# Padding each high weight tile by 96 bytes, so that its five places start at five positions within 512 bytes of SBUF

## The chip, the cores and the metric

The kernel runs on one core of a Trainium2 chip. The metric is the device time of one execution in microseconds (us), lower is better. Three runs of the kernel before gave 1294.0, 1297.97 and 1297.98 us; their median, 1297.97 us, is the time before.

## The reference

A decoder trunk of two layers over 512 tokens of width 1024, all in float32. Layer 0 mixes tokens with stick-breaking attention (16 heads of 64), layer 1 with dilated sliding-window attention (three groups of 8 heads). Behind each mixer stands a gated feed-forward block with a causal convolution of width 3 over 2816 channels. Cut to what matters here, which is that nearly all work is products of activations with weights that are read once:

```python
def reference(x, ...):
    for i in range(DEPTH):                       # 2 layers
        hn = rms_norm(x, norm_gains[i, 0])
        if kind == 0:
            m = stick_breaking_attention(hn, sb_w_qkv[j], sb_w_o[j])     # hn @ w_qkv, ..., o @ w_o
        elif kind == 1:
            m = dilated_attention(hn, dil_w_qkv[j], dil_w_o[j], rel_bias)
        x = x + rms_norm(m, norm_gains[i, 1])
        f = conv_ffn(rms_norm(x, norm_gains[i, 2]), ffn_w_up[i], ffn_conv_w[i],
                     ffn_conv_b[i], ffn_w_down[i])                       # (silu(g) * u) @ w_down
        x = x + rms_norm(f, norm_gains[i, 3])
    return x
```

## The kernel before

Every weight matrix is cut on the host into 204 pieces of 128x1024 float32 (512 KB). A piece goes through class Weights in three steps. `load` fetches it by a DMA of the SP queue into one of three places `wraw`. `split` makes two parts of it: `wh`, the value rounded to the matrix engine's float32r format, by a copy on ACT (L77), and `wl`, the remainder raw minus `wh`, by a subtraction on DVE (L78). Each part has five places in SBUF (`n_high` is 5), which are used in turn. `next` hands a piece to the matmuls, cut along its row into 8 blocks of 128 or 2 blocks of 512 columns, and `done` splits the next piece and starts the load behind it.

A product is made of three matmuls that add into the same PSUM bank, high by high, high by low and low by high:

```python
def mm3(o, sH, sL, mH, mL, first, last):
    nc.tensor.matmul(o, sH, mH, start=first, stop=False)   # L202
    nc.tensor.matmul(o, sH, mL, start=False, stop=False)   # L203
    nc.tensor.matmul(o, sL, mH, start=False, stop=last)    # L204
```

The first operand of a matmul is held in the array: it is loaded ahead of each matmul by a weight load (PEld in the profile, 128x128). The second is streamed through it (512 columns, in one place 256). Two families follow from which side the weights stand on:

- Weights held, activations `hH`, `hL` streamed: `proj_f`, used for the projections to queries and keys (tiles `qk` in layer 0, `dqk` in layer 1) and for the wide half of the feed-forward block (`up`).
- Activations held, weights streamed: the values (`v`, with `hH`, `hL` held; `dv`, with `hH`, `hL` or their regrouped copies `hc` held), the output projections (`o`, `do`, with `oH`, `oL` or `doH`, `doL` held) and the narrow half of the feed-forward block (`dn`, with `gH`, `gL` held).

The program's order is that of the code: the attention of one pair of heads is slipped between the projections of the next, so that the matrix engine always has a projection at hand. The pieces are split several ahead of their use, as far as the five places go.

Tiles of one pool lie behind each other in SBUF. All the large ones have a length of a multiple of 512 bytes per partition, so that tiles of a pool start at the same position within 512 bytes. A row of a 128-column block is 512 bytes, one of 512 columns 2048 bytes, so every block of a tile also starts at that position. In the kernel before, `x`, `hH`, `hL`, `wraw`, `wh`, `wl` and `hc` all start at 352 within 512, and `oH`, `oL`, `doH`, `doL`, `gH`, `gL` at 288.

Of the kernel before, what the change touches and what calls it, by code (L numbers as in the profile page):

```python
# [10 lines left out]
F32 = mybir.dt.float32  # L11
F32R = mybir.dt.float32r
I32 = mybir.dt.int32
AF = mybir.ActivationFunctionType
ALU = mybir.AluOpType
# [3 lines left out]
P = 128  # L19
# [26 lines left out]
class Weights:  # L46
# [22 lines left out]
    def split(self):  # L69
        n = self.splitted  # L70
        if n >= len(self.srcs):
            return
        nc = self.nc
        raw = self.raw.pop(n)
        h = self.pool.tile([P, 1024], F32R, name=f"wh{n}", tag="wh", bufs=self.n_high)
        low = self.pool.tile([P, 1024], F32R, name=f"wl{n}", tag="wl", bufs=self.n_high)
        nc.scalar.copy(h, raw)  # L77
        nc.vector.tensor_tensor(low, raw, h[:].bitcast(F32), op=ALU.subtract)  # L78
        self.parts[n] = (h, low)
        self.splitted += 1  # L80

    def next(self, m):

        n = self.used
        self.used += 1
        h, low = self.parts[n]
        return (
            h[:].rearrange("p (k m) -> p k m", m=m),
            low[:].rearrange("p (k m) -> p k m", m=m),
        )  # L90

    def done(self, later=False):
# [14 lines left out]
def hybrid_trunk_kernel(  # L107
# [275 lines left out]
    with ExitStack() as c2:  # L383
# [7 lines left out]
        r_in = []  # L391
        bias = bias_vectors(ap.tile([P, 2 * 10 * P], F32, name="room", tag="at"))
        next(bias)
        keep_busy(6)
        turned(0, 0, ident, "in0")
# [36 lines left out]

        v_half(0)
        next(bias)
        v_half(1)
        nc.vector.tensor_copy(
# [588 lines left out]
```

## Time and profile before

| what | value |
|---|---|
| median of three runs | 1297.97 us (1294.0 to 1297.98) |
| the profiled execution's own time | 1296.61 us |
| its span, first to last instruction | 1294.8 us |
| TensorE matmul (PE) busy | 1268.5 us, 98% |
| TensorE weight load (PEld) busy | 1024.9 us, 79% |
| VectorE (DVE) busy | 767.8 us, 59% |
| ScalarE (ACT) busy | 554.5 us, 43% |
| mean granted TensorE clock | 0.989 of full speed |

The profiled execution took 1.81 us more than its span, and it lies 1.36 us under the median. A matmul's busy time is longer than its share of the engine, because matmuls overlap in the pipeline and their ends are modelled: the pace of the engine is read from the distance between the starts of two matmuls, in the view of instructions in order of time. That view gives starts in steps of 0.01 us, so a pace is read from two starts that lie far apart and the number of matmuls between them.

### The profile page before, as it was taken

The page shows a single profiled execution, that of the slowest core. Times are in us where ns is not written, and L with a number is a line of the kernel's source. Part 1 is how long each engine was busy: PE and PEld are TensorE (multiplying, and loading weights), DVE is VectorE, ACT ScalarE, POOL GpSimd, SP SyncE. Part 2 cuts the span into 40 slices and gives each one's busy share as a digit, 9 for nine tenths or more (in the row PEclk, how much of TensorE's full clock was granted, in tenths as well). Part 3 has the DMA queues.
Part 4 walks back from the last instruction along what each step waited for, and adds up shares of the span by engine and source line. Part 5 has one row for each costly group of instructions (what it writes and reads, how often), then busy time and mean ns, then how long its engine had stood idle before and what let it go on. Part 6 is the DMA issues. An engine that isn't in the chain of part 4 may idle for free.

```text
span 1294.8 us, 16912 instructions
## 1 busy us (share of the span) xinstructions
PE 1268.5 (98%) x6556; PEld 1024.9 (79%) x6556; DVE 767.8 (59%) x1425; ACT 554.5 (43%) x941; POOL 74.5 (6%) x169
## 2 busy tenths in 40 slices
PE   8998999999999999999999999999999999999997
PEld 6775776788888888888878877777888888888886
DVE  5266788378777777332663354455887777773324
ACT  6445556356444444221455243334654444442210
POOL 1000000000000000000260012300100000000000
PEclk8998999999999999999999999999999999999999
DMA  6541212243323324322463323330433322343311
GB/s 217 105 129 33 66 65 95 75 144 114 98 98 98 98 98 145 116 91 93 131 187 98 98 75 95 88 121 27 150 114 98 98 98 98 96 138 112 95 64 65
DMA packets 39760, 133.48 MB, mean 103 GB/s; under 512 B 6047, under 2 KB 7103, under 8 KB 39680
## 3 DMA queue, kind: packets, MB, share of 16 engines
q1 hardware_dynamic: 32400, 115.37, 27.6%
q0 software_dynamic: 7280, 17.03, 4.8%
q8 instruction: 51, 0.84, 0.3%
q14 instruction: 29, 0.24, 0.1%
HBM read 122.78 MB, written 9.60 MB: 102 GB/s over the span
## 4 chain that ended last, share of the span: by engine, by line
PE 94%; DVE 2%; ACT 2%; issue 1%; DMA 1%; SPq 0%; DVEq 0%; ACTq 0%
PE up L203 12%; PE up L202 12%; PE up L204 12%; PE dn L203 6%; PE dn L202 6%; PE dn L204 6%; PE dqk L202 4%; PE dqk L204 3%; PE dqk L203 3%; PE qk L202 2%; PE qk L204 2%; PE qk L203 2%; PE dv L202 2%; PE dv L204 2%; PE dv L203 2%; PE z L359 2%
## 5 line engine op out<-in xcount | busy, mean ns | idle before, releaser
L78 DVE TENSOR_TENSOR wl<-wraw,wh 128x1024 fp32r<-128x1024 f32 x204 | 249.5, 1224 | 218.5 <-ACT wh L77 215.9
L77 ACT CAST wh<-wraw 128x1024 fp32r<-128x1024 f32 x204 | 214.5, 1051 | 267.0 <-PE dn L204 137.8
L203 PE MATMUL up<-hL,wh 128*128 128x512 f32 (+1 forms) x768 | 285.4, 373 | 2.1 <-DVE hL L269 2.1
L202 PE MATMUL up<-hH,wh 128*128 128x512 f32 (+1 forms) x768 | 284.5, 374 | 1.1 <-ACT hH L268 1.1
L204 PE MATMUL up<-hH,wl 128*128 128x512 f32 (+1 forms) x768 | 284.8, 372 | 0.0
L203 PEld LDWEIGHTS up<-hL,wh 128*128 128x128 f32 x768 | 145.1, 189 | 27.6 <-DVE hL L269 2.8
L202 PEld LDWEIGHTS up<-hH,wh 128*128 128x128 f32 x768 | 143.9, 189 | 27.2 <-ACT hH L268 2.0
L204 PEld LDWEIGHTS up<-hH,wl 128*128 128x128 f32 x768 | 145.1, 189 | 25.2
L203 PE MATMUL dn<-wl,gH 128*128 128x512 f32 x352 | 138.7, 394 | 0.0
L202 PE MATMUL dn<-wh,gH 128*128 128x512 f32 x352 | 138.0, 392 | 0.0
L204 PE MATMUL dn<-wh,gL 128*128 128x512 f32 x352 | 136.6, 388 | 0.0
L607 DVE SCALAR_TENSOR_TENSOR up<-work,cw,up 128x510 f32<-128x510 f32 (+1 forms) x176 | 131.5, 751 | 5.0 <-ACT up L605 2.2
L604 DVE TENSOR_TENSOR work<-up,rows 128x512 f32<-128x512 f32 x88 | 60.1, 687 | 70.6 <-PE up L204 70.6
L202 PEld LDWEIGHTS dn<-wh,gH 128*128 128x128 f32 x352 | 66.1, 188 | 15.4
L202 PE MATMUL dqk<-hH,wh 128*128 128x512 f32 x192 | 77.8, 405 | 0.0
L204 PEld LDWEIGHTS dn<-wh,gL 128*128 128x128 f32 x352 | 66.1, 188 | 14.8
L203 PEld LDWEIGHTS dn<-wl,gH 128*128 128x128 f32 x352 | 66.2, 188 | 13.1
L204 PE MATMUL dqk<-hH,wl 128*128 128x512 f32 x192 | 75.1, 391 | 0.0
L203 PE MATMUL dqk<-hL,wh 128*128 128x512 f32 x192 | 75.0, 391 | 0.0
L605 ACT ACTIVATE up<-work,cb,cw 128x512 f32<-128x512 f32 x88 | 68.6, 781 | 11.6 <-DVE work L604 9.3
L618 ACT CAST gH<-work 128x512 fp32r<-128x512 f32 x44 | 27.2, 618 | 106.7 <-DVE work L617 106.7
L616 ACT ACTIVATE work<-up 128x512 f32<-128x512 f32 x44 | 26.3, 597 | 73.4 <-DVE up L607 73.3
(236 smaller groups left out, 1751.2 us busy)
## 6 DMA issues: line engine op xcount, KB each, us to landing
wraw<-in_up_dram SPq DMA_DIRECT2D x88, 512.0 KB, 3.5
wraw<-in_down_dram SPq DMA_DIRECT2D x44, 512.0 KB, 3.5
wraw<-in_dl_qk_dram SPq DMA_DIRECT2D x24, 512.0 KB, 3.5
wraw<-in_sb_qk_dram SPq DMA_DIRECT2D x16, 512.0 KB, 4.1
wraw<-in_dl_v_dram SPq DMA_DIRECT2D x12, 512.0 KB, 4.1
wraw<-in_sb_v_dram SPq DMA_DIRECT2D x8, 512.0 KB, 5.3
wraw<-in_sb_o_dram SPq DMA_DIRECT2D x8, 512.0 KB, 3.5
x<-x_away POOLq DMA_DIRECT2D x8, 512.0 KB, 3.8
```

What stands on the lines that cost most here:

```text
L77: nc.scalar.copy(h, raw)
L78: nc.vector.tensor_tensor(low, raw, h[:].bitcast(F32), op=ALU.subtract)
L202: nc.tensor.matmul(o, sH, mH, start=first, stop=False)
L203: nc.tensor.matmul(o, sH, mL, start=False, stop=False)
L204: nc.tensor.matmul(o, sL, mH, start=False, stop=last)
L359: nc.tensor.matmul(outs[h], lhs[r, :], rhs[r, :], start=True, stop=True, tile_position=(h * HD, 0))
L604: nc.vector.tensor_tensor(h, o, rows, op=ALU.mult)
L605: nc.scalar.activation(o, h, AF.Identity, bias=cb[:, f : f + 1], scale=cw[:, f, 2:3])
L607: nc.vector.scalar_tensor_tensor(o[:, : S - s], h[:, s:], cw[:, f, 2 - s : 3 - s], o[:, : S - s], op0=ALU.mult, op1=ALU.add,)
L616: nc.scalar.activation(g, og, AF.Silu)
L618: nc.scalar.copy(gH[:, f, :], u)
```

## The change

Each tile `wh` is allocated with 24 more columns (96 bytes) than it holds, and the code uses its first 1024. The rest of the diff moves the slicing `[:]` from the uses to the allocation.

```diff
-        h = self.pool.tile([P, 1024], F32R, name=f"wh{n}", tag="wh", bufs=self.n_high)
-        low = self.pool.tile([P, 1024], F32R, name=f"wl{n}", tag="wl", bufs=self.n_high)
+
+        h = self.pool.tile([P, 1024 + 24], F32R, name=f"wh{n}", tag="wh", bufs=self.n_high)[:, :1024]
+        low = self.pool.tile([P, 1024], F32R, name=f"wl{n}", tag="wl", bufs=self.n_high)[:]
         nc.scalar.copy(h, raw)
-        nc.vector.tensor_tensor(low, raw, h[:].bitcast(F32), op=ALU.subtract)
+        nc.vector.tensor_tensor(low, raw, h.bitcast(F32), op=ALU.subtract)
```

No instruction is added, taken away or moved: on every engine and queue the two programs have the same instructions with the same shapes in the same order, and the same waits. What differs is where tiles start. Positions within 512 bytes of a partition, as the two built programs have them:

| tiles | before | after |
|---|---|---|
| `x`, `qk`, `work`, `hH`, `hL`, `wraw` | 352 | 352 |
| `wh`, five places | 352 each | 352, 448, 32, 128, 224 |
| `wl`, five places | 352 each | 320 each |
| `hc` and the other temporaries, `dqk` of odd pairs | 352 | 320 |
| `oH`, `oL`, `doH`, `doL`, `gH`, `gL`, `v_sb` | 288 | 256 |

All that lies behind the five places of `wh` is 480 bytes further on, which is 32 bytes less within 512.

## Rows read from the trace of the kernel before

**Rows 1.** The page: busy time, share and instructions of each engine; then the chain's engines.
```profile
PE 1268.5 (98%) x6556; PEld 1024.9 (79%) x6556; DVE 767.8 (59%) x1425; ACT 554.5 (43%) x941; POOL 74.5 (6%) x169
...
PE 94%; DVE 2%; ACT 2%; issue 1%; DMA 1%; SPq 0%; DVEq 0%; ACTq 0%
```

**Rows 2.** Who waited for whom, PE alone: us in total, times, longest; the longest row.
```profile
PE o L517 <- ACT at L508: 4.3, 1, 4.3
```

**Rows 3.** Groups by shape: line, engine, tiles, shapes, count | busy us, mean ns | idle before.
```profile
L202 PE MATMUL up<-hH,wh 128*128 128x512 f32 x640 | 249.0, 389 | 0.0
...
L202 PE MATMUL dn<-wh,gH 128*128 128x512 f32 x352 | 138.0, 392 | 0.0
...
L202 PE MATMUL dqk<-hH,wh 128*128 128x512 f32 x192 | 77.8, 405 | 0.0
...
L202 PE MATMUL qk<-hH,wh 128*128 128x512 f32 x128 | 52.6, 411 | 0.0
...
L204 PE MATMUL up<-hH,wl 128*128 128x256 f32 x128 | 35.9, 287 | 0.0
...
L202 PE MATMUL v<-wh,hH 128*128 128x512 f32 x64 | 27.2, 425 | 0.8 <-ACT hH L268 0.8
L202 PE MATMUL o<-wh,oH 128*128 128x512 f32 x64 | 26.3, 411 | 0.0
...
L202 PE MATMUL dv<-wh,hc 128*128 128x512 f32 x64 | 25.2, 394 | 1.6 <-ACT hc L725 1.6
...
L202 PE MATMUL do<-wh,doH 128*128 128x512 f32 x32 | 13.3, 414 | 0.0
L202 PE MATMUL dv<-wh,hH 128*128 128x512 f32 x32 | 12.9, 404 | 0.0
```

**Rows 4.** The same view: the group that makes the low part of the weights.
```profile
L78 DVE TENSOR_TENSOR wl<-wraw,wh 128x1024 fp32r<-128x1024 f32 x204 | 249.5, 1224 | 218.5 <-ACT wh L77 215.9
```

**Rows 5.** Busy time by stretch: stretch, us, PE, PEld, DVE, ACT, POOL, clock, DMA share, GB/s.
```profile
292.00:519.00 227.00, 227.00 (x1033) 189.26 (x1032) 170.37 (x216) 105.67 (x133) 1.63 (x3) 1.00 0.33 107
```

**Rows 6.** Instructions in order of time (start, us each): PE in `up`, first and last of 181.
```profile
330.01 0.39 PE L203 MATMUL up<-hL,wh 128*128 128x512 f32 x1
...
370.81 0.39 PE L203 MATMUL up<-hL,wh 128*128 128x512 f32 x1
```

**Rows 7.** The same view: PE in `dv`, activations `hc` held, first and last of 175.
```profile
669.92 0.39 PE L202 MATMUL dv<-wh,hc 128*128 128x512 f32 x1
...
709.37 0.39 PE L202 MATMUL dv<-wh,hc 128*128 128x512 f32 x1
```

**Rows 8.** The same view: PE in `dn`, first and last of 178.
```profile
559.81 0.39 PE L204 MATMUL dn<-wh,gL 128*128 128x512 f32 x1
...
600.32 0.39 PE L204 MATMUL dn<-wh,gL 128*128 128x512 f32 x1
```

**Rows 9.** The same view: PE in `o`, first and last of 106.
```profile
239.27 0.39 PE L204 MATMUL o<-wh,oL 128*128 128x512 f32 x1
...
263.31 0.39 PE L204 MATMUL o<-wh,oL 128*128 128x512 f32 x1
```

**Rows 10.** The same view: PE in `qk` behind four transposes, first to last of eleven.
```profile
154.60 0.40 PE L203 MATMUL qk<-hL,wh 128*128 128x512 f32 x1
...
155.07 0.39 PE L202 MATMUL qk<-hH,wh 128*128 128x512 f32 x1
155.29 0.39 PE L203 MATMUL qk<-hL,wh 128*128 128x512 f32 x1
...
156.91 0.40 PE L204 MATMUL qk<-hH,wl 128*128 128x512 f32 x1
```

**Rows 11.** The same view: PE in `up` with 256 columns, first and last of 27.
```profile
281.51 0.28 PE L203 MATMUL up<-hL,wh 128*128 128x256 f32 x1
...
284.63 0.28 PE L203 MATMUL up<-hL,wh 128*128 128x256 f32 x1
```

More of the change, by code (lines that the diff above doesn't have):

```diff
@@ L87, in next @@
         return (
-            h[:].rearrange("p (k m) -> p k m", m=m),
-            low[:].rearrange("p (k m) -> p k m", m=m),
+            h.rearrange("p (k m) -> p k m", m=m),
+            low.rearrange("p (k m) -> p k m", m=m),
         )
```

## The prediction, made before the changed kernel ran

> **What bounds the kernel now.** I read four views in this order. The page first: the matrix engine is busy for 98% of the span, and the chain that ended last runs over it for 94% [rows 1]. Then who waited for whom, on PE alone: the longest wait in the whole program is 4.3 us, and it is for an attention tile [rows 2]; no row of that view names L77 or L78, so PE never stands still for a split weight piece. Third, the groups by shape: nearly all of PE's work is one shape, a 128x128 operand held and 512 columns streamed [rows 3]. Last, the instructions in order of time, because a matmul's busy time (about 390 ns) overlaps its neighbours and only the distance of the starts tells the pace.
>
> That last view holds what this change can touch. In the middle of `up`, 180 distances take 370.81 - 330.01 = 40.80 us: **226.7 ns** a matmul [rows 6]. In `dv`, with the weights on the other side, 174 distances take 39.45 us: 226.7 ns again [rows 7]. In `dn`, 177 take 40.51 us: **228.9 ns** [rows 8]; in `o`, 105 take 24.04 us: 229.0 ns [rows 9]. [...] What sets them apart goes with the position of the operands within 512 bytes: in `up`, `v` and `dv` the held and the streamed operand both start at 352; in `dn`, `o` and `do` the held one starts at 288, 64 bytes earlier. The side on which the weights stand does not matter (`dv` has them streamed, as `dn` has, and keeps the pace of `up`). So equal positions go with 226.7 ns and a difference of 64 bytes with 228.9. No other difference occurs in this kernel.
>
> A third pace appears behind a disturbance. After four transposes, eleven `qk` matmuls with equal positions start between 154.60 and 156.91: ten distances in 2.31 us, **231 ns** each, and single distances swing [rows 10]. Equal positions need some matmuls to settle into 226.7.
>
> [...] With 256 columns 26 distances take 3.12 us, 120.0 ns, which is 106.7 + 13.3 [rows 11]: the extra is a fixed amount for each matmul, not one for each column.
>
> **The change part by part.** Nothing is added, removed or reordered, so there are no instructions to price, only positions.
>
> The splitting on ACT and DVE (L77, L78) writes and reads at new positions. Whatever that does to its 1224 ns [rows 4], it is hidden: the DVE group stood idle for 218.5 us ahead of its 204 runs, over 1 us each, and PE never waited for it [rows 2]. Without that cover, 10% on 249.5 us would be 25 us; PE's list shows the cover whole: I take zero. The loads still land in `wraw` at 352.
>
> The operands of the matmuls are the whole matter. I count them from [rows 3], three lines for each group.
>
> 1. Positions equal before: `up` 1920, `dqk` 576, `qk` 384, `v` 192, `dv` 192 and 96, together 3360 of 512 columns, and 384 of 256 columns in `up`. After the change the differences between `wh` and its activation are 0, 96, 192, 288 or 384 bytes by the place, and for `wl` it is 32 bytes. Only one place in five stays equal, and within each group of three matmuls the held or streamed position jumps between that of `wh` and that of `wl`. The trace has no row for these differences. The nearest rows are the one other difference that occurs, +2.2 ns (228.9 against 226.7), and the unsettled pace, +4.3 ns (231). On the other side stands the shortest single distance, 155.07 to 155.29, 0.22 us [rows 10], some 6.7 ns below 226.7, and as a floor the bare columns, 13.3 ns below. I take +2.2 ns, the settled pace of unequal positions: 3360 x 2.2 = 7.4 us, and with the same on the 384 short ones 0.8 us, **+8.2 us**. The place that stays equal could spare about 1 us of it. Ends: 3360 x 4.3 = +14.4 us and 3360 x -6.7 = -22.5 us.
> 2. Positions already unequal: `dn` 1056, `o` 192, `do` 96, together 1344. They go from one difference of 64 bytes to six different ones (64 for `wl`, and 32, 96, 128, 192 and 224 for the places of `wh`). I take **zero**. Ends: back to the pace of equal positions, 1344 x -2.2 = -3.0 us; up to the unsettled pace, 1344 x 2.1 = +2.8 us; and with the shortest distance, 1344 x -8.9 = -12 us.
>
> Sum: +8.2 us. On the profiled execution's own 1296.61 us that is 1304.8; on the median, 1.36 us higher, 1306.2.
>
> [...]
>
> **The rivals.**
>
> *Nothing that can be measured.* The two paces could have another cause than position: `gH` and `oH` also lie higher in SBUF than `hH` and `hc`, and the held tile is what the two families differ in. Then the places of `wh` are free to move. For it: DVE is busy for 170 and ACT for 106 of the 227 us that hold most of `up` [rows 5], and the pace there is the best one, so PE's reads seem robust against what else goes on in SBUF. Against it: `o`, `do` and `dn` are three different tiles and share the one difference of 64 bytes. Time: 1298, or 1295 if `dn` and `o` settle as `up` does. [...]
>
> *Faster, because the fixed 13.3 ns are a collision.* The held operand of the next matmul is loaded while the present one streams. If both reads start at the same position within 512 bytes they may meet in the same part of the memory, and the fixed extra of each matmul [rows 6, 11] would be the price of meeting, paid once for each weight load. Moving the places apart would lift part of it. For it: the extra doesn't depend on the columns, and it shows in equal positions. Against it: the one difference that occurs, 64 bytes, costs more and not less [rows 8, 9]. It decides as soon as the mean over 4704 matmuls falls by more than 0.8 ns (3.9 us). Its far end in rows is the 0.22 us distance, -22.5 - 12 = -34.5 us; half of that, as the places differ among themselves, gives about **1281**.
>
> [...]
>
> *Slower by more, because it never settles.* With equal positions a disturbed sequence takes about ten matmuls to settle [rows 10]. When the position jumps in every group of three, it might never do so: 231 ns everywhere, +14.4 + 2.8 = +17 us, **1315**.
>
> **How the numbers follow.** About 0.3% (3.9 us) is what a measurement of this kernel can tell from no change. Chances: the forecast, +4 to +12 us, 0.40; never settling 0.12; nothing measurable 0.21; faster 0.27. Most of the weight is on slower because the only two departures from the settled equal pace that the trace shows, 228.9 and 231, both lie above it; it isn't more because five of the six new differences have no row. So slower 0.51, with a little of the forecast's lower end given to same, same 0.22, faster 0.27. The predicted time is that of the likeliest case, 1306. The range leaves out the farther half of the faster case (0.12) and the far end of never settling (0.06): 1283 to 1316. The likeliest case alone would be 1302 to 1310.
>
> **What would show it.** In the changed kernel's trace the distance of starts in `up` should be about 229 ns where it was 226.7, differ from piece to piece with the place of `wh` (one piece in five nearer to the old pace), and stay near 229 in `dn`. If `up` is still at 226.7, position isn't the cause of the two paces. If it falls below 226, the collision is real and the forecast has the wrong sign. L77 and L78 should stay absent from PE's waits. I would be wrong on the first step if the paces go with the height of a tile in SBUF, and on the second if some differences are far better than equal.

## The result, and the profile after

The changed kernel takes **1313.88 us** (median of four runs, 1312.41 to 1314.78) where the kernel before takes 1296.93 (four runs). The ratio is 1.0135, 95% interval 1.0121 to 1.0149: 17 us slower. The forecast was slower, 1306, with a range from 1283 to 1316. The sign is right and the range holds the time; the size is about double.

The profiled execution took 1314.78 us. Its page differs from that of before by more than 3 us in one thing only, 17.6 us of PE:

```profile
span 1313.0 us, 16912 instructions
...
PE 1286.1 (98%) x6556; PEld 1026.0 (78%) x6556; DVE 769.3 (59%) x1425; ACT 551.7 (42%) x941; POOL 74.4 (6%) x169
...
PE 94%; DVE 2%; ACT 2%; DMA 1%; issue 1%; SPq 0%; DVEq 0%; ACTq 0%
```

The counts and the shares of the chain are those of [rows 1]. Who waited for whom on PE begins as in [rows 2] and again names neither the rounding nor the subtraction (now L78 and L79); the group that makes the low part takes the same 1224 ns as in [rows 4], and stood idle for 223.7 us ahead of its runs:

```profile
PE o L518 <- ACT at L509: 4.3, 1, 4.3
```
```profile
L79 DVE TENSOR_TENSOR wl<-wraw,wh 128x1024 fp32r<-128x1024 f32 x204 | 249.5, 1224 | 223.7 <-ACT wh L78 223.2
```

So the cover holds, and nearly all of the time lies in the pace of the matmuls. In order of time (start, us each), PE in `up`, first and last of 177, which answer to [rows 6]:

```profile
330.01 0.40 PE L205 MATMUL up<-hH,wl 128*128 128x512 f32 x1
...
370.89 0.39 PE L204 MATMUL up<-hL,wh 128*128 128x512 f32 x1
```

176 distances in 40.88 us are 232.3 ns, 5.6 more than before. And in `dn`, first and last of 178, which answer to [rows 8]: 41.00 us / 177 = 231.6 ns, 2.8 more.

```profile
559.91 0.40 PE L205 MATMUL dn<-wh,gL 128*128 128x512 f32 x1
...
600.91 0.40 PE L205 MATMUL dn<-wh,gL 128*128 128x512 f32 x1
```

The granted clock was not the cause. The stretch that answers to [rows 5] has it at 1.00 again, with fewer matmuls in the same 227 us:

```profile
296.00:523.00 227.00, 227.00 (x1000) 184.94 (x999) 168.53 (x213) 100.45 (x129) 1.62 (x3) 1.00 0.34 105
```

Within one piece of weights the pace is strictly regular. Here is PE in the middle of a piece that lies at 448, in order of time:

```profile
429.90 0.40 PE L203 MATMUL up<-hH,wh 128*128 128x512 f32 x1
430.14 0.39 PE L204 MATMUL up<-hL,wh 128*128 128x512 f32 x1
430.37 0.40 PE L205 MATMUL up<-hH,wl 128*128 128x512 f32 x1
430.60 0.40 PE L203 MATMUL up<-hH,wh 128*128 128x512 f32 x1
430.84 0.39 PE L204 MATMUL up<-hL,wh 128*128 128x512 f32 x1
431.07 0.40 PE L205 MATMUL up<-hH,wl 128*128 128x512 f32 x1
431.30 0.40 PE L203 MATMUL up<-hH,wh 128*128 128x512 f32 x1
```

Each group of three takes 0.70 us, again and again. This is no sequence that fails to settle: it settles, at a slower pace than 0.68 us.

By the places of `wh`, the mean distance in `up`, from the first start of a piece to the first of the next (24 distances), 16 pieces for a place (before: 226.7 in all):

| place of `wh` | 352 | 448 | 32 | 128 | 224 |
|---|---|---|---|---|---|
| ns a matmul | 231.2 | 233.3 | 233.4 | 231.2 | 232.4 |

Even the place that `wh` never left, 352, is slow.

### The profile page after: what moved, and what is told of

It reads as the page before. It is cut to its first block, busy times and chain, and to the rows that moved or that the text cites. A ratio compares the mean times of both kernels' runs of the same rounds, so it can differ in the third digit from the quotient of the medians.

```text
span 1313.0 us, 16912 instructions
## 1 busy us (share of the span) xinstructions
PE 1286.1 (98%) x6556; PEld 1026.0 (78%) x6556; DVE 769.3 (59%) x1425; ACT 551.7 (42%) x941; POOL 74.4 (6%) x169
## 4 chain that ended last, share of the span: by engine, by line
PE 94%; DVE 2%; ACT 2%; DMA 1%; issue 1%; SPq 0%; DVEq 0%; ACTq 0%
PE up L205 12%; PE up L203 12%; PE up L204 12%; PE dn L205 6%; PE dn L204 6%; PE dn L203 6%; PE dqk L203 4%; PE dqk L205 3%; PE dqk L204 3%; PE qk L203 2%; PE qk L205 2%; PE qk L204 2%; PE dv L203 2%; PE dv L205 2%; PE z L360 2%; PE dv L204 2%
## 5 line engine op out<-in xcount | busy, mean ns | idle before, releaser
L79 DVE TENSOR_TENSOR wl<-wraw,wh 128x1024 fp32r<-128x1024 f32 x204 | 249.5, 1224 | 223.7 <-ACT wh L78 223.2
L78 ACT CAST wh<-wraw 128x1024 fp32r<-128x1024 f32 x204 | 213.9, 1048 | 283.4 <-PE dn L205 140.0
L203 PE MATMUL up<-hH,wh 128*128 128x512 f32 (+1 forms) x768 | 288.1, 379 | 1.2 <-ACT hH L269 1.2
L205 PE MATMUL up<-hH,wl 128*128 128x512 f32 (+1 forms) x768 | 288.3, 376 | 0.0
```

Source lines behind the costliest of these rows:

```text
L79: nc.vector.tensor_tensor(low, raw, h.bitcast(F32), op=ALU.subtract)
```

## The experiments

The theory, in short *difference*: what counts is how far the held and the streamed operand of the matmuls lie apart within 512 bytes, and only equal positions give 226.7 ns. The rivals: *jumps* (it costs that the position changes between `wh` and `wl`), *absolute position or height in SBUF*, and *collision* (some distance is better than none). Where a text below says "as before", tiles start where they do in the kernel before. Where SBUF had no room for a gap, the two small tiles of the convolution's weights were put into one, which frees 32 bytes; no instruction changes by it.

**The two halves of the change, apart.** The change moves the five places of `wh`, and it moves all that lies behind them by 480 bytes. First the places alone, on top of the changed kernel:

```diff
+        if n == 0:
+            self.pool.tile([P, 8], F32, name="gap", tag="gap", bufs=1)
         low = self.pool.tile([P, 1024], F32R, name=f"wl{n}", tag="wl", bufs=self.n_high)[:]
```

> The five places of wh as in the changed kernel (352, 448, 32, 128, 224), but a gap of 32 bytes behind them brings wl, hc, oH, gH and the rest back to where they were (352 and 288). Theory of the difference (a settled 226.7 ns needs held and streamed operand at equal positions in all three matmuls of a group): up falls out of step in four pieces of five, about 231 to 232 ns there, 226.7 in the place at 352, because wl is equal again; up as a whole 230 to 231, the kernel 1308 to 1312. Rival, it is the move of wl and of what lies behind it: up stays at 226.7 and the kernel at 1297 to 1299.

Measured: 1309.94 us against 1296.15, ratio 1.011 (1.0097 to 1.0123), inside the expected band; the four places that differ spread wider than the 231 to 232 ns expected. In `up` the place at 352 had 227.4 ns, the others 228.9 (32), 230.3 (448), 231.4 (128) and 233.9 (224). The place at 224, first and 22nd matmul of one piece (4.91 us / 21 = 233.8 ns), and the place at 352 (4.77 / 21 = 227.1):

```profile
409.79 0.40 PE L205 MATMUL up<-hH,wh 128*128 128x512 f32 x1
...
414.70 0.39 PE L205 MATMUL up<-hH,wh 128*128 128x512 f32 x1
...
431.98 0.39 PE L205 MATMUL up<-hH,wh 128*128 128x512 f32 x1
...
436.75 0.39 PE L205 MATMUL up<-hH,wh 128*128 128x512 f32 x1
```

Then the rest alone, on top of the kernel before:

```diff
         h = self.pool.tile([P, 1024], F32R, name=f"wh{n}", tag="wh", bufs=self.n_high)
+        if n == 0:
+            self.pool.tile([P, 120], F32, name="gap", tag="gap", bufs=1)
```

> The five places of wh stay at 352; a gap of 480 bytes behind them moves wl and hc to 320 and oH, gH and the rest to 256, as in the changed kernel. Theory of the difference: every group of three in up now has one held operand 32 bytes off, as the pieces at 352 have in the changed kernel, where they ran at 231.3 ns; up 231 in all pieces, dn near 230, the kernel 1307 to 1312. Rival, the five places do it all: up 226.7, the kernel 1297 to 1299.

Measured: 1313.22 us, ratio 1.0132 (1.0119 to 1.0145), a little above the expected band. With every `wh` at 352 and only `wl` moved by 32 bytes, all pieces of `up` ran at 232.2 ns. First and last of 177 (40.87 us / 176):

```profile
330.01 0.40 PE L206 MATMUL up<-hH,wl 128*128 128x512 f32 x1
...
370.88 0.39 PE L205 MATMUL up<-hL,wh 128*128 128x512 f32 x1
```

Each half costs nearly the whole: +13.8 and +17.1 us alone, +17 together. They don't add. That a group of three which is out of step for one reason loses little more by a second would explain it; no run tests it.

**Difference or jumps.** `wh` and `wl` of a piece share one place, so that nothing jumps within a piece:

```diff
-        h = self.pool.tile([P, 1024 + 24], F32R, name=f"wh{n}", tag="wh", bufs=self.n_high)[:, :1024]
-        low = self.pool.tile([P, 1024], F32R, name=f"wl{n}", tag="wl", bufs=self.n_high)[:]
+        t = self.pool.tile([P, 2048 + 24], F32R, name=f"wh{n}", tag="wh", bufs=self.n_high)
+        h, low = t[:, :1024], t[:, 1024:2048]
+        if n == 0:
+            self.pool.tile([P, 8], F32, name="gap", tag="gap", bufs=1)
```

> wh and wl of a piece share one place, so both start at the same position: 352, 448, 32, 128, 224 by the place; all else as before. Within a piece nothing jumps any more, but wh and wl both differ from the activations by 0, 96, 192, 288 or 384 bytes. Theory of the difference: one place of five at 226.7, the others about 229 as a constant difference of 64 bytes has in dn of the kernel before; the kernel 1302 to 1307. Rival, the jumps between wh and wl cost and not the difference: up 226.7 in every place, the kernel 1296 to 1299.

Measured: 1314.15 us, ratio 1.0136 (1.0123 to 1.015). The rival falls: without any jump the kernel is as slow as the changed one. But my expectation of 229 ns for a constant difference falls too. The place at 352 ran at 227.0 ns, as forecast, and 192 bytes apart (position 32) gave 229.2; 96, 288 and 384 bytes apart gave 234.2, 233.4 and 232.6. At 448, 96 bytes apart, first and 22nd of a piece (4.92 us / 21 = 234.3 ns; the trace calls both parts `wh` here):

```profile
427.72 0.39 PE L205 MATMUL up<-hH,wh 128*128 128x512 f32 x1
...
432.64 0.39 PE L205 MATMUL up<-hH,wh 128*128 128x512 f32 x1
```

**All equal.** The kernel before with 64 bytes more ahead of the stage tiles, so that `gH`, `oH` and the like start at 352 too:

```diff
     rb = const.tile([NB + 1, DG * DH], F32, name="rb")
+    sp.tile([P, 16], F32, name="gap", tag="gap", bufs=1)
```

> The kernel before with 64 bytes more ahead of oH, gH and the other large tiles of the stages, so that they too start at 352, as wh, wl, hH and hL do. Theory of the difference: dn, o and do go from 228.9 to 226.7 ns, 1344 x 2.2 = 3.0 us, the kernel 1293 to 1295. Rival, those stages have their pace from the height of the tiles in SBUF or from being other tiles: dn stays at 228.9, the kernel 1297.

Measured: 1293.5 us against 1296.15, ratio **0.9979** (0.9971 to 0.9988): small, but with 12 runs against 17 clear of noise, so this version beats both kernels. Over all its back-to-back matmuls `o` went from 229.2 to 227.7 ns; in `dn`, first and last of 182, 41.03 us / 181 = 226.7 ns:

```profile
559.95 0.39 PE L203 MATMUL dn<-wl,gH 128*128 128x512 f32 x1
...
600.98 0.39 PE L204 MATMUL dn<-wh,gL 128*128 128x512 f32 x1
```

Then everything at position 0:

```diff
     rb = const.tile([NB + 1, DG * DH], F32, name="rb")
+    const.tile([P, 40], F32, name="lead", tag="lead")
+    sp.tile([P, 16], F32, name="gap", tag="gap", bufs=1)
```

> All large tiles start at position 0 within 512 bytes (160 bytes more ahead of x, 64 more ahead of oH and gH): all equal, as in the run with everything at 352, but at another absolute position. Theory of the difference: up and dn both at 226.7 ns, the kernel 1292 to 1295. Rival, a start at a multiple of 512 or 64 bytes is itself faster (one memory line less for each block): up below 226, the kernel under 1285; or 352 is a lucky position: up above 228, the kernel over 1300.

Measured: 1293.82 us against 1296.02, ratio 0.998 (0.997 to 0.9989), `up` and `dn` both at 226.7 ns. The absolute position does not count, and a start at a multiple of 512 bytes gains nothing by itself. Height does not count either: in both runs `gH` lies above `hH` as it did, and runs at the pace of `hH`.

**Is another distance better than none?** Three kernels, run once each, cover the distances in steps of 32 bytes, with the shared tile of the run above, a padding of 16 or 8 columns and a gap of 0, 8 or 80 columns ahead:

```diff
+        if n == 0:
+            self.pool.tile([P, 80], F32, name="lead", tag="lead", bufs=1)
+        t = self.pool.tile([P, 2048 + 8], F32R, name=f"wh{n}", tag="wh", bufs=self.n_high)
+        h, low = t[:, :1024], t[:, 1024:2048]
```

> A look at the pace by difference: wh and wl of a piece share a place, the five places start 0, 64, 128, 192 and 256 bytes behind hH and hL within 512 bytes; what lies behind the weights moves too (to 160 and 96) and is not compared. Theory of the difference: up in the place at 0 226.7 ns, at 192 229 as measured before, at 64, 128 and 256 229 to 234. Rival, that some differences are better than equal, as reads that avoid each other would be: one of them under 226 ns.

> The same with the five places 32, 96, 160, 224 and 288 bytes behind hH and hL. Theory of the difference: at 96 234, at 288 233.4 as measured before with the same differences, at 32, 160 and 224 229 to 234. Rival: one of them under 226 ns.

> The same with the five places 320, 352, 384, 416 and 448 bytes behind hH and hL. Theory of the difference: at 384 232.6 as measured before, at 448 (64 bytes ahead) 228.9 as dn had in the kernel before with the held side 64 bytes ahead, the others 229 to 234. Rival: one of them under 226 ns.

Measured: 1306.16, 1317.82 and 1316.31 us against 1296.02. The settled pace in `up` by how many bytes the held operand (`wh`, `wl`) starts behind the streamed one (`hH`, `hL`) within 512. Each value is the mean of the 6th to the 20th distance of the starts in 16 pieces; the run with shared places above is used too (384 bytes, 232.3), and where two runs have a value that differs, both stand:

| held behind streamed, bytes | ns | 256 more | ns |
|---|---|---|---|
| 0 | 226.7 | 256 | **226.7** |
| 32 | 233.2 | 288 | 233.2 |
| 64 | 233.5 | 320 | 233.2 |
| 96 | 234.5, 234.3 | 352 | 234.3 |
| 128 | 232.3 | 384 | 233.6, 232.3 |
| 160 | 233.3 | 416 | 233.3 |
| 192 | 228.9 | 448 | 228.9 |
| 224 | 233.3 | 480 | not run |

No distance is better than 0. The two columns agree: positions count within **256** bytes, not 512. The first of the three shows it best; here the place 256 bytes apart and then the one 64 bytes apart, first and 22nd matmul each (4.76 us / 21 = 226.7 ns, 4.89 / 21 = 232.9):

```profile
410.58 0.39 PE L203 MATMUL up<-hH,wh 128*128 128x512 f32 x1
...
415.34 0.39 PE L203 MATMUL up<-hH,wh 128*128 128x512 f32 x1
...
427.11 0.39 PE L203 MATMUL up<-hH,wh 128*128 128x512 f32 x1
...
432.00 0.40 PE L203 MATMUL up<-hH,wh 128*128 128x512 f32 x1
```

The settled distances repeat after two to seven matmuls, so a mean over 15 of them can be off by some tenths; over whole repeats 32, 64, 160, 224, 288, 320 and 416 all give 233.3, 96 and 352 give 234.3, and 128 gives 232.4.

Of all the distances in the table that are not 0 or 256, only 192 and 448 are mild. In these the held operand starts 64 bytes ahead of the streamed one, counted within 256, which is just what `dn` and `o` have in the kernel before (288 against 352): the one example that its trace offered was the best of the bad ones.

The same runs hold the map with the weights on the streamed side. In the last 12 or 14 distances of its pieces `dn` has 226.7 ns at 0 and 256 bytes, 228.9 at 192, 233.3 at 32, 64, 160 and 224, 232.4 at 128 and 234.3 at 96.

Not every distance has one settled pace, though. In the first of the three runs the place at 128 bytes settled at 232.4 ns in 15 of its pieces of `up` and at 233.3 in one. And with 448 bytes, where `dn` in the kernel before keeps 228.9, six pieces of `dn` in the run with shared places, each behind a piece at 352 bytes, stay at 233.3, and so do six in the run with the places alone. First and 22nd of one in the run with shared places (4.90 us / 21 = 233.3):

```profile
572.23 0.40 PE L205 MATMUL dn<-wh,gH 128*128 128x512 f32 x1
...
577.13 0.40 PE L205 MATMUL dn<-wh,gH 128*128 128x512 f32 x1
```

So the distance alone does not fix the pace of unequal positions; what ran just before seems to count too, since the same place in the same kernel could settle either way.

**Does 256 hold on the other side too?** The kernel before with 320 bytes ahead of the stage tiles, `gH` and `oH` at 96, 256 from the weights that are streamed there:

```diff
     rb = const.tile([NB + 1, DG * DH], F32, name="rb")
+    sp.tile([P, 80], F32, name="gap", tag="gap", bufs=1)
```

> The kernel before with 320 bytes more ahead of oH, gH and the other stage tiles, so that they start at 96, exactly 256 bytes from wh and wl. Theory that positions count within 256 bytes, from the places 256 bytes apart that kept 226.7 ns in up: dn, o and do at 226.7 with the weights on the streamed side too, the kernel 1292 to 1295 as with all equal. Rival, positions count within 512 bytes and the place at 256 was an exception of up: dn at 228.9 or more, the kernel 1296 or more.

Measured: 1293.62 us against 1295.88, ratio 0.998 (0.997 to 0.9989). `dn` again at 226.7, first and last of 182 (41.03 us / 181):

```profile
559.93 0.39 PE L202 MATMUL dn<-wh,gH 128*128 128x512 f32 x1
...
600.96 0.39 PE L203 MATMUL dn<-wl,gH 128*128 128x512 f32 x1
```

**How equal must it be?** `hH` and `hL` in one tile, read from its column 4 or 7, while the weights lie 32 bytes (8 columns) further on:

```diff
-    hH = xp.tile([P, KD, S], F32R, name="hH")
-    hL = xp.tile([P, KD, S], F32R, name="hL")
+    hb = xp.tile([P, 2 * KD * S + 8], F32R, name="hb")
+    hH, hL = (hb[:, 4 + n * KD * S : 4 + (n + 1) * KD * S].rearrange("p (k s) -> p k s", k=KD)
+              for n in range(2))
```

> hH and hL start 16 bytes (4 numbers) ahead of wh and wl within 512 bytes; oH, gH and the rest keep their 64 bytes of difference to the weights. Theory of the difference, as a matter of small steps: up no longer settles, 229 to 234 ns, as every multiple of 32 other than 0 and 256 gave. Rival, operands within the same 32 bytes count as equal: up 226.7.

> The same with hH and hL 4 bytes (one number) ahead of wh and wl. Theory of the difference with a tolerance: up 226.7 to 227.5 ns. Rival, equality must be exact: up 229 or more.

Measured: 1318.04 and 1304.45 us against 1295.88, one run each. 16 bytes apart gave 236.6 ns in `up`, the slowest of all and above the 229 to 234 expected; a single number, 4 bytes, gave 230.6 (231.1 by the measure of the table, as the first distances of a piece are shorter), so the tolerance that I had expected isn't there. `dn`, whose operands kept their 64 bytes, stayed at 228.9 in both. In these two runs alone the streamed tiles start at no multiple of 32 bytes (368 and 380); whether that start by itself costs something, beside the distance, is not tested. First and last of 174 with 16 bytes (40.95 us / 173 = 236.7), and of 178 with 4 bytes (40.81 / 177 = 230.6):

```profile
329.90 0.40 PE L203 MATMUL up<-hb,wh 128*128 128x512 f32 x1
...
370.85 0.40 PE L205 MATMUL up<-hb,wl 128*128 128x512 f32 x1
```
```profile
330.05 0.40 PE L204 MATMUL up<-hb,wh 128*128 128x512 f32 x1
...
370.86 0.40 PE L204 MATMUL up<-hb,wh 128*128 128x512 f32 x1
```

## Why the prediction was right, and where its size was off

**What bounds the kernel.** Right. Nearly all of the change is in PE's pace, and neither DVE nor ACT was ever waited for on account of a weight piece.

**The cause of the two paces.** Right, though the trace could not prove it: it showed one difference, and height and the other tiles went with it. The run with all equal shows it from the other side, since moving the stage tiles by 64 bytes alone brought `dn` from 228.9 to 226.7 and the kernel down by the 3.0 us that the second step's end gave (measured 2.65, interval 1.6 to 3.8).

**Step 1, the positions that were equal: the term that was mis-sized.** I priced them with +2.2 ns, the one settled example, where `up` measured +5.6. Summed from start to start, waits included, `up` grew by 10.7 us, `dqk` by 1.9, `qk` by 0.9, `dv` by 1.9 (0.6 of it a longer wait for `hc`, 2.2 us for 1.6), and `v` fell by 0.5: 14.9 us where the step had 7.4. `v` is no exception: back to back at full clock it slowed from 227.6 to 232.3 ns, but its first matmuls ran at a granted clock of 0.50, where five distances before the change take 2.13 us (13.10 to 15.23), 426 ns each, and the clock reached 1.00 sooner. From 11 to 20 us it was 0.76 on the mean, before the change 0.63. Two things were wrong. I took the difference in `dn` as typical, and the map shows that it is the mildest there is; most multiples of 32 bytes cost 6 to 8 ns. And the place that stays equal, which I thought might spare 1 us, spared nothing, because `wl` beside it had moved by 32 bytes. A slip of less weight: the step gave the regrouped `hc` the differences of `hH`, though `hc` moves to 320 with `wl`.

**The 384 short matmuls** in `up` were forecast at +0.8 us and fell by 1.0 us. With 256 columns equal positions are not the best but among the slowest: where all three matmuls of a group are 0 or 256 bytes apart they settle at 120.0 ns in every run [rows 11], while the last 12 distances of an undisturbed piece have means from 113.3 to 120.0 at the other positions. The lowest in steady repeat is that of the pieces 448 bytes apart in the last of the three kernels above, first and 22nd of one (2.38 us / 21 = 113.3):

```profile
944.58 0.28 PE L205 MATMUL up<-hH,wh 128*128 128x256 f32 x1
...
946.96 0.28 PE L205 MATMUL up<-hH,wh 128*128 128x256 f32 x1
```

Why the two widths differ is open. The prediction's 106.7 and 13.3 ns follow from two rows: 256 columns more take 226.7 - 120.0 = 106.7 ns, and 13.3 are left of 120.0 [rows 6, 11]. An estimate from `v` at the granted clock of 0.50 comes to the same: half of its 426 ns is 213, about twice 106.7. That these 13.3 ns are a fixed amount for each matmul was an estimate from those two widths at equal positions, and the 113.3 ns end it: taking off the same 106.7 leaves 6.7.

**Step 2, the positions that were unequal.** Forecast zero, measured +3.5 us (`dn` 3.0, `o` 0.4, `do` 0.1), a bit above the upper end of 2.8. It follows from the map: `dn` left one of the two mild distances.

Together 14.9 - 1.0 + 3.5 = 17.4 of the 18.2 us by which the span grew. The prediction's signs failed by the same term: `up` was to be near 229 and was 232.3, `dn` was to stay near 229 and was 231.6.

**The range.** That it holds the time is in part luck. The likeliest case alone would have been 1302 to 1310, which 1313.88 misses; the range reached 1316 for a rival whose mechanism is not what the runs show.

**The rivals.** *Nothing measurable* is refuted by the result, and its reason, height, by the two runs with all equal. The settled pace of one and the same shape ran from 226.7 to 236.6 ns by position alone. *Collision* starts from held operands that are loaded while matmuls stream, and these do overlap: PEld is busy for 79% of the span and PE for 98% [rows 1]. In the form that equal positions are the meeting point it is refuted for 512 columns by the map, where no distance goes below 226.7; the 256-column matmuls do go the way that it said, with 113.3 to 120.0 ns against 120.0. What the 13.3 ns are, is left open. *Never settling* had nearly the right time, 1315, and the wrong reason: the matmuls do settle, within a piece and with a strict repeat of three or six, but at a slower pace.

## What to carry to other kernels

Where a stream of 128x512 float32r matmuls bounds a kernel, look at the distance of their starts by stage; if it differs, compare where the held and the streamed tiles start within 256 bytes. For this shape, lay all tiles that meet in a matmul at the same position modulo 256 bytes (226.7 ns here, against 228.9 to 236.7); for 256 columns that is not the best position (120.0 ns, against 113.3 to 120.0), so measure it. A padding that seems free can cost over 1% (1.35% here), and one line of padding that restores the equality gave 0.2% here. And where a trace offers a single example of a deviation, take it as one draw and keep the range open to worse ones.

## What the runs showed of the hardware that was not expected

The pace of back-to-back float32r matmuls of 512 columns depends on how far the held operand starts behind the streamed one, modulo 256 bytes. It does not matter on which side the weights stand, nor, where all are equal, at which of the two absolute positions tried: 226.7 ns at 0, 228.9 at 192 (233.3 in 12 pieces of `dn`, at 448), 232 to 234.5 at the other multiples of 32. With a start off the multiples of 32 it was 231.1 at 4 bytes and 236.7 at 16. With 256 columns it was 120.0 at 0 and 256, and from 113.3 to 120.0 at the others.

The settled distances go in steps. In `up` they repeat in every trace after one to nine matmuls, and the sum over one whole repeat is on the mean within 0.1 ns of a multiple of 6.67 ns: 226.7 (34 steps) for one matmul at distance 0, 466.7 (70) for two at 32, 686.7 (103) for three at 192, 700.0 (105) for three at 160, 1640.0 (246) for seven at 96; with 256 columns 120.0 (18) and 113.3 (17) for one. So the starts seem to be held to some regular beat, which would fit that a disturbed sequence needs several matmuls to fall into step, as the ten distances of 231 ns behind four transposes suggest [rows 10]. What beats, no run here shows.
